# The decays' scalars and the modulation blocks move into the first three convolution groups, and the first key block is listed ahead of the decays

## The chip, the core and the metric

One NeuronCore of a Trainium2 chip runs the whole kernel in one launch. The metric is the device time of one execution in microseconds (us). TensorE (PE in the profile), VectorE (DVE), ScalarE (ACT) and GpSimd (POOL) each take their instructions in order; SyncE (SP) issues nearly all transfers, also in order. All arithmetic is float32; the projections run as three passes over a high and a low part of each operand.

## The reference, cut to what matters

One layer of a hybrid backbone, for 1024 latent tokens and 256 context tokens of width 1024:

```
mod   = silu(c) @ w_mod + b_mod                       # 6 x 1024: shift, scale, gate, twice
u     = modulate(rmsnorm(x), sh1, sc1) @ w_in         # q k v | z | b a | conformer channels
beta  = sigmoid(b);  g = -exp(a_log) * softplus(a + dt_bias)
q,k,v = silu(conv7(q,k,v)); q,k l2-normed             # 4 heads of 128
o     = gated DeltaNet over chunks, forward and backward, decays exp(sums of g)
y     = silu(layernorm(conv31 along grid columns(a * sigmoid(b'))))
x     = x + gt1 * (concat(gated_norm(o, z), y) @ w_out)
x     = x + gt2 * moe(modulate(rmsnorm(x), sh2, sc2)) # 64 experts, top 6, and a shared one
out   = rmsnorm(x) * g_final
```

## The kernel before, in words

Up to line 448 the instructions are traced in program order and a list scheduler places them: program order is priority, and what is ready may go ahead. `mod_block` (line 270) multiplies 512 columns of `w_mod` (`mod_product`, 250; 2.1 MB per block, from block 4 on through two buffers), copies the product (`ms`, 259), transposes it (265) and adds the bias (267, 268). Blocks 0 to 3 are done before the tokens are modulated. Then a loop over four groups j of 128 conformer channels (422) projects each group in two halves (`cf_project`, 368; `fm`, 314, is one projection of 24 products per 512 tokens), loads the next group's weights (`load_cf`), does two modulation blocks, 4+2j and 5+2j, and for j below 3 the 31 taps of the grid convolution (`grid_tap`, 412; tap 15 starts the sum on ScalarE, 415, the others are VectorE's, 419). After the loop the gates are laid into `gtc`, transposed, and stored to `gt_d` (434 to 448).

From line 488 on the order is planned: each step is listed with an engine, a planned duration, what it reads and writes (by names), and `Order.emit` (105) plays these through, always giving a free engine the ready step with the longest path behind it (`low` steps after all others). What is emitted is the order in each engine's queue; between the part before and this part the list scheduler still interleaves. Names of buffers and PSUM banks are dealt out in turn when a step is listed (`turn_of`, `bbank`: banks 4 to 7 in turn), so the listing decides who waits for whose buffer. The first planned part contains:

- `o_scalars` (582): two parameter loads, sigmoid and softplus of the 80 gate scalars per token on ScalarE and VectorE (587 to 601), running sums on TensorE (608 to 612), their exponentials `eg` (615), a transpose (617) and the store `egr_d` (620). Its result `gg` feeds every decay.
- `o_grid_conv(3)`: the last group's grid convolution.
- `o_decays(c)` (629) for ten chunks: masked copies of `gg` on GpSimd (637) and ScalarE (635), running sums on TensorE (643), an Exp (646), a store.
- `o_norm_half` (534): the layer norm of the conformer channels, in two halves.
- `o_qkv(blk)` (716): load and split of one weight block (683 on ScalarE, 684 on GpSimd; staging in three buffers, split parts in two, four after `open_prep`), the projection (697), copies into `cx` (723, 726), seven taps (744 on ScalarE, 746 or 710 on VectorE), Silu (752), transposes (763), and for keys the squares and their sums (767 to 769). Blocks 4 to 7 are keys, 8 to 11 values, 0 to 3 queries. `o_z` (778) is a projection without taps.
- `o_masks` (831): block masks on GpSimd and VectorE, with `low=1`.
- `o_key_norms` (649), `o_prep1` (883: products of keys, 892, times decay factors, 897 to 901), `o_spread` (911), `o_base_inverse` (924: 15 steps on VectorE, 937 and 938, on copies held in `qf`), then `o_conv_out` (786) and `o_query_norms` (952). `open_prep` closes the pool of the convolution and opens the next one.

A second planned part follows: inverses, the scan over chunks, output projection, routing and shared expert; then the routed experts, whose weights are loaded once the router's expert list is there (fetch, lines 1752 to 1775).

Of the kernel before, what the change touches and what calls it, by code (L numbers as in the profile page):

```python
# [8 lines left out]
F32 = mybir.dt.float32  # L9
# [4 lines left out]
OP = mybir.AluOpType  # L14
# [135 lines left out]
def hybrid_kernel(tc, a, out):  # L150
# [270 lines left out]

    for j in range(4):
# [12 lines left out]
    gt_d = dp.tile([32, 128], F32, name="gt_d")  # L435
    pt = bank("b")
    gtc = cfp.tile([128, 32], F32, name="gtc")
    V.tensor_copy(gtc[:, 0:8], MC[:, 16:24, 0])
    V.tensor_copy(gtc[:, 8:16], MC[:, 40:48, 0])
    for i in range(2):  # L440
        V.tensor_copy(gtc[:, 16 + 8 * i:24 + 8 * i], sv['mf'][i])
    PE.transpose(pt[0:32, 0:128], gtc, ident)
    gtr = cfp.tile([32, 128], F32, name="gtr")
    V.tensor_copy(gtr, pt[0:32, 0:128])
    SY.dma_start(gt_d, gtr)

    mf8 = cp.tile([128, 2, 8], F32, name="mf8")
    SY.dma_start(mf8, gt_d[16:32].rearrange("(a b) c -> a (b c)", a=2).rearrange("a (p k) -> p a k", k=8))
# [21 lines left out]
    egr_d = dp.tile([80, 128], F32, name="egr_d")  # L470
# [87 lines left out]

    rk = keep.tile([128, 10, 4], F32, name="rk")
    ssk = keep.tile([128, 10, 4], F32, name="ssk")  # L560
    ssq = keep.tile([128, 8, 4], F32, name="ssq")
    alb = keep.tile([128, 2, 8], F32, name="alb")
    bav = bat.rearrange("p c (d w h) -> p w d c h", d=2, w=2)

    def sct(name):
        return keep.tile([128, 2, 10, 4], F32, name=name)

    beta, gg = sct("beta"), sct("gg")
    tmp = lnp.tile([128, 2, 10, 4], F32, name="tmp")
    egr = lnp.tile([80, 128], F32, name="egr")  # L570
    eg = keep.tile([128, 3, 2, 10, 4], F32, name="eg")
    egc, egl = eg[:, 0], eg[:, 2]
# [5 lines left out]

    def per_dh(t):
        return t.rearrange("p (d h) -> p d h", d=2)[:, :, None, :].to_broadcast([128, 2, 10, 4])  # L580

    def o_scalars():
        DMA(0.3, lambda: SY.dma_start(alb[:, 0], w['dn_a_log'].rearrange("d h -> (d h)").partition_broadcast(128)),
            w=["alb0"])
        DMA(0.3, lambda: SY.dma_start(alb[:, 1], w['dn_dt_bias'].rearrange("d h -> (d h)").partition_broadcast(128)),
            w=["alb1"])
        ACT(0.3, lambda: S.activation(beta, bav[:, 0], AF.Sigmoid), w=["beta"])
        DVE(0.3, lambda: V.tensor_tensor(gg, bav[:, 1], per_dh(alb[:, 1]), op=OP.add), r=["alb1"], w=["gs"])

        def softplus():  # L590
            S.activation(tmp, gg, AF.Abs)
            S.activation(tmp, tmp, AF.Exp, scale=-1.0)
            S.activation(alb[:, 0], alb[:, 0], AF.Exp)
            S.activation(tmp, tmp, AF.Ln, bias=1.0)

        ACT(4.0, softplus, r=["alb0"], w=["gs"])

        def decay():
            V.scalar_tensor_tensor(gg, gg, 0.0, tmp, op0=OP.max, op1=OP.add)
            V.tensor_tensor(gg, gg, per_dh(alb[:, 0]), op=OP.mult)  # L600
            V.tensor_scalar(gg, gg, -1.0, None, op0=OP.mult)

        DVE(0.7, decay, w=["gs", "gg"])
        b, kb = bbank()

        def sums():
            ggf = gg.rearrange("p d c h -> p d (c h)")
            PE.matmul(b[:, 0:40], Ui, ggf[:, 0], start=True, stop=True)
            PE.matmul(b[:, 40:80], Li, ggf[:, 1], start=True, stop=True)
            PE.matmul(b[:, 80:120], Ls, ggf[:, 0], start=True, stop=True)  # L610
            PE.matmul(b[:, 120:160], Us, ggf[:, 1], start=True, stop=True)
            PE.matmul(b[:, 160:240], ones, gg.rearrange("p d c h -> p (d c h)"), start=True, stop=True)

        TE(1.2, sums, r=["gs"], w=[kb])
        ACT(1.7, lambda: S.activation(eg.rearrange("p a d c h -> p (a d c h)"), b[:, :240], AF.Exp), r=[kb], w=["eg"])
        b2_, kb2 = bbank()
        TE(0.2, lambda: PE.transpose(b2_[0:80, 0:128], egc.rearrange("p d c h -> p (d c h)"), ident), r=["eg"],
           w=[kb2])
        DVE(0.25, lambda: V.tensor_copy(egr, b2_[0:80, 0:128]), r=[kb2], w=["egr"])
        DMA(0.3, lambda: SY.dma_start(egr_d, egr), r=["egr"], w=["egrd"])  # L620

        DVE(0.3, lambda: V.tensor_reduce(Ic, ident.rearrange("p (b c) -> p c b", c=16), axis=AX.X, op=OP.add), w=["ic"])
# [6 lines left out]
    def o_decays(c):  # L629
# [7 lines left out]
        POOL(1.5, lambda: G.tensor_tensor(RR[u], bm(Ui), b3(gg[:, 0, c]), op=OP.mult), r=["gg"], w=[f"rr{u}"])  # L637
# [32 lines left out]
    def o_load_w(src, k=8, by=None, kby=None):  # L670
# [4 lines left out]
        for i in range(0, k, k // 2):  # L675
# [8 lines left out]
            POOL(1.5, lambda st=st, sl=sl: G.tensor_tensor(lo(sl), st, hi(sl).bitcast(F32), op=OP.subtract),  # L684
# [31 lines left out]
    def o_qkv(blk):  # L716
# [33 lines left out]
        for t in range(1, 7):  # L750
            DVE(1.7, lambda t=t: tap(t), r=[kc], w=[kd])
# [34 lines left out]
    def o_conv_out():  # L786

        wt = []
        for hf in range(2):
            hs_ = slice(hf * 512, (hf + 1) * 512)  # L790
            DMA(0.8, lambda hf=hf: SY.dma_start(flat(DM[hf]), gt_d[4 * hf:4 * hf + 4].rearrange("k p -> (k p)")
                                                .partition_broadcast(128)), w=[f"dm{hf}"])
            wt.append([o_load_w(w['w_out'].rearrange("(k p) n -> p k n", p=128)[:, 4 + 2 * i:6 + 2 * i, hs_], 2,
                                lambda hf=hf: flat(DM[hf]), f"dm{hf}") for i in range(2)])
        for t in range(8):
# [8 lines left out]
            POOL(1.5, lambda hs=hs, parts=parts: G.tensor_tensor(parts()[1], hs, parts()[0].bitcast(F32),  # L804
# [26 lines left out]
    def o_masks():  # L831
# [10 lines left out]
        POOL(1.8, blocks, w=["bd"], low=1)  # L842
# [10 lines left out]
        for s in (16, 32, 64):  # L853
            DVE(1.3, lambda s=s: level(s), r=["bd"], w=[f"m{s}"], low=1)
# [28 lines left out]
    def o_prep1(n):  # L883
        bounce = BN[n]
        for ci, c in enumerate(pairs[n]):
# [14 lines left out]
            POOL(1.5, lambda d=d: G.tensor_tensor(N.NB, N.NB, DM[d], op=OP.mult), r=[f"dm{d}"], w=["nb"])  # L900
# [23 lines left out]
    def o_base_inverse(n):  # L924
# [15 lines left out]
        for m0 in range(0, 15, 3):  # L940
            DVE(2.3, lambda m0=m0: steps(m0, m0 + 3), r=[*kr, "ic"], w=["xf"])
# [43 lines left out]

    def o_grid_conv(j):
        kw = [f"y{j}0", f"y{j}1"]
        ACT(1.2, lambda: grid_tap(j, 15), w=kw)
# [5 lines left out]
    TE(14.0, lambda: None)  # L994
    ACT(6.0, lambda: None)
    POOL(0.6, pads, w=["cx0", "cx1"])
    o_scalars()
    o_grid_conv(3)
    for c in pairs[0]:
        o_decays(c)  # L1000
    for c in pairs[1]:
        o_decays(c)
    for c in pairs[2]:
        o_decays(c)
    for c in pairs[3]:
        o_decays(c)
    for c in pairs[4]:
        o_decays(c)
    o_norm_half(0)
    o_norm_half(1)  # L1010
    o_qkv(4 + 0)
    o_qkv(4 + 1)
    o_qkv(4 + 2)
    o_qkv(4 + 3)
    o_masks()
    once(open_prep, w=["prep", "rv", "gs", "egr", "bd", *(f"rr{i}" for i in range(4)), *(f"y{j}{hf}" for j in range(4) for hf in range(2))])
# [21 lines left out]
    o_z(3)
# [1070 lines left out]
```

## Time and profile before

| | us |
|---|---|
| median of 3 runs | 1730.98 (1727.82 to 2079.73) |
| the profiled execution | 1729.29 |
| its span, first to last instruction | 1727.5 |
| TensorE busy in it | 1604.0 |
| VectorE, GpSimd, ScalarE busy | 977.9, 522.6, 485.3 |

The profile is of one execution. Busy time is of instructions that compute; transfers and waits are not in it. The span is shorter than the time by what lies before the first and behind the last instruction.

### The profile page before, as it was taken

The page shows a single profiled execution, that of the slowest core. Times are in us where ns is not written, and L with a number is a line of the kernel's source. Part 1 is how long each engine was busy: PE and PEld are TensorE (multiplying, and loading weights), DVE is VectorE, ACT ScalarE, POOL GpSimd, SP SyncE. Part 2 cuts the span into 40 slices and gives each one's busy share as a digit, 9 for nine tenths or more (in the row PEclk, how much of TensorE's full clock was granted, in tenths as well). Part 3 has the DMA queues.
Part 4 walks back from the last instruction along what each step waited for, and adds up shares of the span by engine and source line. Part 5 has one row for each costly group of instructions (what it writes and reads, how often), then busy time and mean ns, then how long its engine had stood idle before and what let it go on. Part 6 is the DMA issues. An engine that isn't in the chain of part 4 may idle for free. (4 is left out here: it accounts for less than half of the span.)

```text
span 1727.5 us, 23370 instructions
## 1 busy us (share of the span) xinstructions
PE 1604.0 (93%) x8380; PEld 936.3 (54%) x8380; DVE 977.9 (57%) x2156; ACT 485.3 (28%) x1085; POOL 522.6 (30%) x443
## 2 busy tenths in 40 slices
PE   5999699986998999899999999999999999999994
PEld 1556456865875899788544434344444344443441
DVE  2588865889775985878702444444444434343424
ACT  4521445742232112444212111112121112111212
POOL 2321331162222776732011222323232323232310
PEclk9999899988999999899999999999999999999998
DMA  9455121364525336666358999999999999999957
GB/s 322 152 181 173 32 86 49 112 188 141 184 72 175 96 98 196 216 208 223 140 221 292 340 325 333 315 363 316 322 380 362 333 334 319 321 385 350 353 131 250
DMA packets 150657, 405.38 MB, mean 235 GB/s; under 512 B 21360, under 2 KB 64781, under 8 KB 125581
## 3 DMA queue, kind: packets, MB, share of 16 engines
q1 hardware_dynamic: 130978, 340.39, 54.2%
q0 software_dynamic: 18288, 59.26, 14.5%
q10 hardware_dynamic: 1274, 4.23, 0.6%
q8 instruction: 66, 1.08, 0.2%
q14 instruction: 51, 0.41, 0.1%
HBM read 340.01 MB, written 71.95 MB: 238 GB/s over the span
## 5 line engine op out<-in xcount | busy, mean ns | idle before, releaser
L1607 PE MATMUL gu<-wg,hg 128*32 128x512 f32 (+2 forms) x1968 | 463.2, 599 | 1.8 <-ACT hg L1861 1.8
L1886 DVE SCALAR_TENSOR_TENSOR ob<-dn,wc,gt2b 128x512 f32<-128x512 f32 x124 | 93.1, 751 | 366.0 <-PE dn L1627 366.0
L1895 POOL DMA_INDIRECT acc<-ob,ic x89 | 134.5, 1512 | 527.5 <-DVE st L1817 467.1
L1607 PEld LDWEIGHTS gu<-wg,hg 128*32 128x32 f32 (+2 forms) x1968 | 148.4, 137 | 204.3 <-issue 159.2
L1627 PE MATMUL dn<-wd,sg 128*32 128x512 f32 (+2 forms) x984 | 226.8, 597 | 0.5 <-ACT sg L1618 0.5
L1861 ACT ACTIVATE hg<-xt,mf 128x128 f32<-128x128 f32 x248 | 93.2, 456 | 377.6 <-PE xt L1855 376.0
L1627 PEld LDWEIGHTS dn<-wd,sg 128*32 128x32 f32 (+2 forms) x984 | 77.8, 137 | 143.5 <-issue 142.7
L697 PE MATMUL bk<-hTh,whi 128*128 128x512 f32 (+1 forms) x320 | 127.3, 398 | 8.4 <-ACT ot L783 4.3
L697 PE MATMUL bk<-hTh,wlo 128*128 128x512 f32 (+1 forms) x320 | 121.2, 379 | 0.5 <-POOL wlo L684 0.5
L697 PE MATMUL bk<-hTl,whi 128*128 128x512 f32 (+1 forms) x320 | 121.4, 379 | 0.0
L1859 DVE TENSOR_SCALAR hg<-xt,mf 128x128 f32<-128x128 f32 x248 | 84.3, 402 | 52.1 <-DMA acc<-hg 52.0
L419 DVE SCALAR_TENSOR_TENSOR ycv<-yg,cfw,ycv 128x64 f32<-128x64 f32 (+14 forms) x120 | 107.6, 896 | 5.3 <-ACT ycv L415 2.0
L684 POOL TENSOR_TENSOR wlo<-wst,whi 128x512 fp32r<-128x512 f32 x40 | 65.3, 1637 | 134.1 <-ACT whi L683 134.1
L1845 POOL DMA_INDIRECT xg<-xn_d,ig x62 | 76.6, 1236 | 65.1 <-issue 19.7
L697 PEld LDWEIGHTS bk<-hTh,whi 128*128 128x128 f32 x320 | 62.1, 194 | 32.9 <-issue 11.6
L1806 DVE TENSOR_TENSOR oh<-posl 128x1024 bf16<-128x1024 f32 (+3 forms) x89 | 77.6, 897 | 0.0
L1855 PE MATMUL xt<-ident,xg 128*128 128x128 f32 x496 | 70.3, 285 | 0.0
L697 PEld LDWEIGHTS bk<-hTh,wlo 128*128 128x128 f32 x320 | 62.0, 194 | 12.6 <-POOL wlo L684 0.9
L697 PEld LDWEIGHTS bk<-hTl,whi 128*128 128x128 f32 x320 | 62.1, 194 | 11.5 <-issue 1.4
L1612 DVE TENSOR_TENSOR sg<-sg,gu 128x256 f32<-128x256 f32 x62 | 26.1, 421 | 63.6 <-ACT sg L1611 63.6
L1611 ACT ACTIVATE sg<-gu 128x256 f32<-128x256 f32 x62 | 23.8, 383 | 135.1 <-PE gu L1607 135.1
L1855 PEld LDWEIGHTS xt<-ident,xg 128*128 128x128 f32 x496 | 60.3, 194 | 1.4 <-issue 1.4
(444 smaller groups left out, 2661.1 us busy)
## 6 DMA issues: line engine op xcount, KB each, us to landing
wg<-exp_w_gate SPq DMA_DIRECT2D x64, 1024.0 KB
wg<-exp_w_up SPq DMA_DIRECT2D x64, 1024.0 KB
wd<-exp_w_down SPq DMA_DIRECT2D x64, 1024.0 KB
wm<-w_mod SPq DMA_DIRECT2D x24, 1024.0 KB
wst<-w_in SPq DMA_DIRECT2D x48, 256.0 KB
kv<-kv_d SPq DMA_DIRECT2D x20, 512.0 KB
qf<-bounce SPq DMA_DIRECT2D x20, 256.0 KB
eb<-egr_d SPq DMA_DIRECT2D x18, 256.0 KB
```

The costliest lines, as they stand in the source:

```text
L419: V.scalar_tensor_tensor(yc[:, lo:hi], yg[:, lo + d:hi + d], cfw[:, t * 4 + j:t * 4 + j + 1], yc[:, lo:hi], op0=OP.mult, op1=OP.add)
L684: POOL(1.5, lambda st=st, sl=sl: G.tensor_tensor(lo(sl), st, hi(sl).bitcast(F32), op=OP.subtract), r=[ks_, kh_], w=[kl_])
L697: PE.matmul(b[:, :n], l(k), r[:, k, t0:t0 + n], start=(k == 0 and i == 0), stop=(k == 7 and i == 2))
L1607: PE.matmul(pgu[o:o + n, :].rearrange("p (a f) -> p a f", a=2), lhsT(k, o, n), wts[r][0][:, :, k, :], start=(k == 0), stop=(k == 7), tile_ ...
L1627: PE.matmul(pd[o:o + n, :], aT[:, k, o:o + n], wts[r][1][:, k, hf * 512:(hf + 1) * 512], start=(k == 0), stop=(k == 1), tile_position=(0, ...
L1806: V.tensor_tensor(oh[:, :, o:o + n], N.iol[:, None, p0:p0 + n].to_broadcast([128, 8, n]), N.posr[:, :, r:r + 1].to_broadcast([128, 8, n]), ...
L1845: G.indirect_dma_start(out=xg, out_offset=None, in_=xn_d, in_offset=bass.IndirectOffsetOnAxis(ap=ig, axis=0), bounds_check=1023, oob_is_er ...
L1855: PE.transpose(pt[:, csl(q)], nth(B['xg'][:, 0:1024], 4 * j + q, 8), ident)
L1859: V.tensor_scalar(hg[:, k, :], pt[:, csl(q)], sc_[:, k:k + 1], sh_[:, k:k + 1], op0=OP.mult, op1=OP.add)
L1861: S.activation(hg[:, k, :], pt[:, csl(q)], AF.Identity, scale=sc_[:, k:k + 1], bias=sh_[:, k:k + 1])
L1886: V.scalar_tensor_tensor(ob[:, hs_], res[hf], B['wc'], N.gt2b[:, hs_], op0=OP.mult, op1=OP.mult)
L1895: G.indirect_dma_start(out=acc_d[turn[0]], out_offset=bass.IndirectOffsetOnAxis(ap=ic[:n], axis=0), in_=B['ob'][o:o + n], in_offset=None, ...
```

## The change

`o_scalars` is no longer planned: the same instructions are a function `scalars()` called in the loop's group j=1, ahead of its modulation blocks. Blocks 4 to 11 are done as 4, 5, 6 / 7, 8, 9 / 10, 11 / none. The gates become a listed step `o_gates` that waits for the first key block (`kf0`), and so do the masks, now without `low`. Two empty steps stand for TensorE's and VectorE's remaining work ahead of the plan. Key blocks, decays and norms are listed in another order, and so are some value, z and preparation steps. Planned durations of some steps are changed.

```diff
+    def scalars():
+        SY.dma_start(alb[:, 0], ...)
+        SY.dma_start(alb[:, 1], ...)
+        S.activation(beta, bav[:, 0], AF.Sigmoid)
+        V.tensor_tensor(gg, bav[:, 1], per_dh(alb[:, 1]), op=OP.add)
+        S.activation(tmp, gg, AF.Abs)
+        S.activation(tmp, tmp, AF.Exp, scale=-1.0)
+        S.activation(alb[:, 0], alb[:, 0], AF.Exp)
+        S.activation(tmp, tmp, AF.Ln, bias=1.0)
...
+        b = bank("b")
...
+        S.activation(eg.rearrange("p a d c h -> p (a d c h)"), b[:, :240], AF.Exp)
+        b2_ = bank("b")
+        PE.transpose(b2_[0:80, 0:128], egc.rearrange("p d c h -> p (d c h)"), ident)
+        V.tensor_copy(egr, b2_[0:80, 0:128])
+        SY.dma_start(egr_d, egr)
...
-        for n in (4 + 2 * j, 5 + 2 * j):
+        if j == 1:
+            scalars()
+        for n in ((4, 5, 6), (7, 8, 9), (10, 11), ())[j]:
             mod_block(n)
...
-    scale_shift('mf', 'g_ffn', 32, 24, 0)
-    pt = bank("b")
-    gtc = cfp.tile([128, 32], F32, name="gtc")
...
-    SY.dma_start(gt_d, gtr)
-    SY.dma_start(mf8, ...)
...
-        POOL(1.5, ...)                # decays, weight splits, factors, output parts
+        POOL(1.6, ...)
-            DVE(1.7, lambda t=t: tap(t), r=[kc], w=[kd])
+            DVE(1.6 if kind == 1 else 1.9, lambda t=t: tap(t), r=[kc], w=[kd])
-        POOL(1.8, blocks, w=["bd"], low=1)
+        DVE(0.3, lambda: V.tensor_reduce(Ic, ...), r=["kf0"], w=["ic"])
+        POOL(1.8, blocks, r=["kf0"], w=["bd"])
-            DVE(1.3, lambda s=s: level(s), r=["bd"], w=[f"m{s}"], low=1)
+            DVE(1.3, lambda s=s: level(s), r=["bd"], w=[f"m{s}"])
-            DVE(2.3, lambda m0=m0: steps(m0, m0 + 3), r=[*kr, "ic"], w=["xf"])
+            DVE(2.8, lambda m0=m0: steps(m0, m0 + 3), r=[*kr, "ic"], w=["xf"])
+    def o_gates():
...
+        DVE(0.7, columns, r=["kf0"], w=["gtc"])
+        TE(0.3, lambda: PE.transpose(b[0:32, 0:128], gtc, ident), r=["gtc"], w=[kb])
+        DVE(0.3, lambda: V.tensor_copy(gtr, b[0:32, 0:128]), r=[kb], w=["gtr"])
+        DMA(0.3, lambda: SY.dma_start(gt_d, gtr), r=["gtr"], w=["gtd"])
+        DMA(0.3, lambda: SY.dma_start(mf8, ...), r=["gtd"])
...
-        ACT(1.2, lambda: grid_tap(j, 15), w=kw)
+        ACT(1.2, lambda: grid_tap(j, 15), r=["yg"], w=kw)
-    TE(14.0, lambda: None)
-    ACT(6.0, lambda: None)
+    TE(7.0, lambda: None, w=["yg"])
+    DVE(0.7, lambda: None, w=["yg"])
-    o_scalars()
```

The listing, before and after (D are the decays of a pair, N the norm halves, K, V, Q the blocks of `o_qkv`, P `o_prep1`, S `o_spread`, I `o_base_inverse`, Z `o_z`):

```
before: scalars, grid 3, D0 D1 D2 D3 D4, N0 N1, K0 K1 K2 K3, masks | P0 S0 P1 S1 V0 P2 V1 P3
        V2 I0 S2 V3 Z0 I1 S3 Z1 I2 Z2 I3 Z3 Q0 P4 S4 Q1 I4 Q2 Q3
after:  grid 3, K0, D0 D1, N0 N1, K1, gates, D2, K2, D3, K3, masks, D4 | P0 S0 P1 S1 V0 P2 V1 P3
        I0 V2 S2 Z0 I1 S3 V3 Z1 I2 P4 S4 Z2 I3 Q0 I4 Z3 Q1 Q2 Q3
```

## Rows read from the trace of the kernel before

**Rows 1.** The page: the span, part 1 (busy us, share of the span, instructions) and, from part 2, the DMA share in tenths in 40 equal slices.

```profile
span 1727.5 us, 23370 instructions
...
PE 1604.0 (93%) x8380; PEld 936.3 (54%) x8380; DVE 977.9 (57%) x2156; ACT 485.3 (28%) x1085; POOL 522.6 (30%) x443
...
DMA  9455121364525336666358999999999999999957
```

**Rows 2.** The table by stretch (us): busy us of each engine with its instructions, mean granted clock of TensorE (1 is the full clock), share of the 16 DMA engines, GB/s.

```profile
183.20:202.90 19.70, 6.12 (x43) 1.98 (x42) 13.14 (x44) 9.04 (x15) 3.13 (x8) 0.71 0.06 15
202.90:338.70 135.80, 133.94 (x587) 92.31 (x587) 92.27 (x85) 78.93 (x147) 34.17 (x23) 0.98 0.26 79
338.70:431.00 92.30, 69.07 (x336) 57.42 (x336) 83.76 (x121) 34.84 (x62) 41.75 (x24) 0.87 0.58 163
431.00:556.00 125.00, 122.72 (x504) 93.12 (x504) 83.99 (x142) 37.60 (x60) 30.95 (x21) 0.98 0.43 140
960.00:1000.00 40.00, 40.00 (x256) 15.95 (x252) 15.79 (x48) 6.88 (x19) 9.94 (x7) 1.00 1.00 334
```

**Rows 3.** TensorE's timeline around the end of the last group: start us, us from the first start to the last end, line, operation, tiles, shapes, count, and in brackets the idle time before it and who ended it.

```profile
183.17 2.76 PE L256 MATMUL a<-wm,csil 128*32 128x512 f32 x18
185.87 0.66 PE L265 MATMUL b<-ident,ms 128*128 128x128 f32 x4
186.46 1.92 PE L256 MATMUL a<-wm,csil 128*32 128x512 f32 x14
189.14 0.66 PE L265 MATMUL b<-ident,ms 128*128 128x128 f32 x4 [0.77 <-ACT ms L259]
190.55 0.28 PE L442 MATMUL b<-ident,gtc 128*32 128x128 f32 x1 [0.75 <-DVE gtc L439]
202.89 0.62 PE L608 MATMUL bk<-gg,Ui 128*128 128x40 f32 x2 [12.06 <-DVE gg L601]
...
204.59 0.69 PE L612 MATMUL bk<-gg,ones 128*128 128x80 f32 x2
205.02 0.77 PE L697 MATMUL bk<-hTh,whi 128*128 128x512 f32 x1
```

**Rows 4.** VectorE's timeline in the same stretch, same columns (the lines left out between the grid taps are those of the masks, 848 to 851).

```profile
192.37 0.23 DVE L588 TENSOR_TENSOR gg<-bat,alb 128x80 f32<-128x80 f32 x1
192.52 0.48 DVE L419 SCALAR_TENSOR_TENSOR ycv<-yg,cfw,ycv 128x256 f32<-128x256 f32 x1
...
194.25 0.54 DVE L419 SCALAR_TENSOR_TENSOR ycv<-yg,cfw,ycv 128x320 f32<-128x320 f32 x1
...
195.98 0.61 DVE L419 SCALAR_TENSOR_TENSOR ycv<-yg,cfw,ycv 128x384 f32<-128x384 f32 x1
...
198.84 3.24 DVE L419 SCALAR_TENSOR_TENSOR ycv<-yg,cfw,ycv 128x448 f32<-128x448 f32 x4
202.00 0.23 DVE L599 SCALAR_TENSOR_TENSOR gg<-gg,tmp 128x80 f32<-128x80 f32 x1
...
202.54 0.20 DVE L601 TENSOR_SCALAR gg<-gg 128x80 f32<-128x80 f32 x1
```

**Rows 5.** ScalarE's timeline: the softplus with its function-table loads, and the first Silu of the planned part.

```profile
192.93 1.28 ACT L592 ACT_TABLE_LOAD   x1
194.22 0.27 ACT L592 ACTIVATE tmp<-tmp 128x80 f32<-128x80 f32 x1
...
195.90 0.27 ACT L594 ACTIVATE tmp<-tmp 128x80 f32<-128x80 f32 x1
...
256.85 1.28 ACT L752 ACT_TABLE_LOAD   x1
```

**Rows 6.** The table by stretch behind the wait, columns as in rows 2.

```profile
202.90:206.00 3.10, 3.10 (x12) 2.93 (x13) 3.03 (x3) 3.08 (x9) 3.10 (x2) 0.50 0.00 0
206.00:209.00 3.00, 3.00 (x8) 1.91 (x7) 2.96 (x2) 1.42 (x3) 3.00 (x3) 0.60 0.00 0
209.00:212.00 3.00, 3.00 (x10) 1.45 (x9) 2.93 (x3) 2.01 (x6) 3.00 (x2) 1.00 0.47 109
```

**Rows 7.** TensorE's timeline at the modulation blocks of the first three groups: the transposes of a block (265) with their waits, and the product of the first group's second block (256).

```profile
93.79 0.66 PE L265 MATMUL b<-ident,ms 128*128 128x128 f32 x4 [0.23 <-ACT ms L259]
94.38 1.92 PE L256 MATMUL a<-wm,csil 128*32 128x512 f32 x14
...
125.23 0.65 PE L265 MATMUL b<-ident,ms 128*128 128x128 f32 x4 [3.76 <-ACT ms L259]
...
156.60 0.66 PE L265 MATMUL b<-ident,ms 128*128 128x128 f32 x4 [3.02 <-ACT ms L259]
```

**Rows 8.** The table by stretch while the two blocks of the second group are loaded, columns as in rows 2.

```profile
93.00:96.50 3.50, 3.27 (x23) 1.30 (x22) 2.15 (x7) 1.87 (x3) 0.00 (x0) 1.00 0.59 174
96.50:100.00 3.50, 3.50 (x18) 2.85 (x18) 2.70 (x8) 0.45 (x1) 0.00 (x0) 1.00 1.05 397
```

**Rows 9.** TensorE's instructions in 338.7 to 431 grouped by line: count, busy us and mean ns of one, idle time before them and who ended most of it.

```profile
L763 PE MATMUL bk<-ident,ac 128*128 128x128 f32 x40 | 7.8, 339 | 14.7 <-DVE tm L937 6.3 <-DVE ot L772 4.3 <-DVE wt L901 2.4
```

**Rows 10.** VectorE's groups in 331 to 431: the taps of the value blocks, columns as in rows 9.

```profile
L746 DVE SCALAR_TENSOR_TENSOR ac<-cx,cnv,ac 128x1283 f32<-128x1283 f32 x24 | 46.1, 1948 | 2.6 <-ACT ac L744 2.5
```

**Rows 11.** VectorE's groups in 183 to 340: the taps of the key blocks and of the last grid convolution.

```profile
L746 DVE SCALAR_TENSOR_TENSOR kf<-cx,cnv,kf 128x1283 f32<-128x1283 f32 x24 | 37.7, 1583 | 20.2 <-ACT kf L744 19.9
L419 DVE SCALAR_TENSOR_TENSOR ycv<-yg,cfw,ycv 128x64 f32<-128x64 f32 (+14 forms) x30 | 32.6, 1085 | 0.8
```

More of the change, by code (lines that the diff above doesn't have):

```diff
@@ L577, in hybrid_kernel @@
     Ic = gbase.tile([128, 16], F32, name="Ic")
[L579 to L622, printed above, removed]
@@ L840, in blocks @@
                                 channel_multiplier=-1)
-        POOL(1.8, blocks, w=["bd"], low=1)
+        DVE(0.3, lambda: V.tensor_reduce(Ic, ident.rearrange("p (b c) -> p c b", c=16), axis=AX.X, op=OP.add),
+            r=["kf0"], w=["ic"])
+        POOL(1.8, blocks, r=["kf0"], w=["bd"])
         def level(s):
@@ L984, in pads, with columns @@
                 G.memset(cx[:, z0:z0 + 3], 0.0)
+    def o_gates():
+        gtc = lnp.tile([128, 32], F32, name="gtc")
+        gtr = lnp.tile([32, 128], F32, name="gtr")
+        def columns():
+            scale_shift('mf', 'g_ffn', 32, 24, 0)
+            V.tensor_copy(gtc[:, 0:8], MC[:, 16:24, 0])
+            V.tensor_copy(gtc[:, 8:16], MC[:, 40:48, 0])
+            for i in range(2):
+                V.tensor_copy(gtc[:, 16 + 8 * i:24 + 8 * i], sv['mf'][i])
+        DVE(0.7, columns, r=["kf0"], w=["gtc"])
+        b, kb = bbank()
+        TE(0.3, lambda: PE.transpose(b[0:32, 0:128], gtc, ident), r=["gtc"], w=[kb])
+        DVE(0.3, lambda: V.tensor_copy(gtr, b[0:32, 0:128]), r=[kb], w=["gtr"])
+        DMA(0.3, lambda: SY.dma_start(gt_d, gtr), r=["gtr"], w=["gtd"])
+        DMA(0.3, lambda: SY.dma_start(mf8, gt_d[16:32].rearrange("(a b) c -> a (b c)", a=2)
+                                      .rearrange("a (p k) -> p a k", k=8)), r=["gtd"])
     def o_grid_conv(j):
         kw = [f"y{j}0", f"y{j}1"]
-        ACT(1.2, lambda: grid_tap(j, 15), w=kw)
+        ACT(1.2, lambda: grid_tap(j, 15), r=["yg"], w=kw)
         for t in range(31):
@@ L1002, in hybrid_kernel @@
         o_decays(c)
+    o_norm_half(0)
+    o_norm_half(1)
+    o_qkv(4 + 1)
+    o_gates()
     for c in pairs[2]:
         o_decays(c)
+    o_qkv(4 + 2)
     for c in pairs[3]:
         o_decays(c)
+    o_qkv(4 + 3)
+    o_masks()
     for c in pairs[4]:
         o_decays(c)
[L1009 to L1016, printed above, removed]
+    once(open_prep, w=["prep", "rv", "gtc", "gtr", "bd", *(f"rr{i}" for i in range(4)), *(f"y{j}{hf}" for j in range(4) for hf in range(2))])
     N.wbufs, turns["w"], turns["ot"] = 4, -1, 0
@@ L1026, in hybrid_kernel @@
     o_prep1(3)
+    o_base_inverse(0)
     o_qkv(8 + 2)
-    o_base_inverse(0)
     o_spread(2)
-    o_qkv(8 + 3)
     o_z(0)
@@ L1033, in hybrid_kernel @@
     o_spread(3)
+    o_qkv(8 + 3)
     o_z(1)
     o_base_inverse(2)
+    o_prep1(4)
+    o_spread(4)
     o_z(2)
     o_base_inverse(3)
+    o_qkv(0)
+    o_base_inverse(4)
     o_z(3)
-    o_qkv(0)
-    o_prep1(4)
-    o_spread(4)
     o_qkv(1)
-    o_base_inverse(4)
     o_qkv(2)
```

58 lines of the change are left out of this document (32 added, 26 removed).

## The prediction

> **What bounds the kernel now.** I read the page's busy shares first: TensorE is busy 1604.0 of 1727.5 us, VectorE 57%; and in the slices the DMA share is high only in the last half [rows 1]. So there are two kernels in one. The table by stretch says which is which: from 960 us on DMA runs at 1.00 of its engines, and before that TensorE is the fullest engine, with one hole: in 183.2 to 202.9 it is busy for 6.12 of 19.70 us, at a mean granted clock of 0.71. In 202.9 to 338.7 it is busy 133.94 of 135.80 and in 431 to 556 122.72 of 125.00; between them, 338.7 to 431, it is busy only 69.07 of 92.30, and there VectorE, with 83.76, is the fuller [rows 2]. The change works in the hole and reorders the stretches behind it. The reader should see that what is saved there reaches the end: TensorE is full in 431 to 556, the second planned part starts when that is done, and expert loads need the router's result, so all that comes later moves as one block.
>
> In the hole, TensorE's own timeline shows two modulation blocks (products 183.17 and 186.46, transposes 185.87 and 189.14), one transpose for the gates at 190.55, then 12.06 us of nothing until L608, released by VectorE's L601 [rows 3]. VectorE reaches L588 at 192.37 and L599 only at 202.00: the softplus on ScalarE was done at about 196.2, but in VectorE's order masks and seven grid taps stood ahead of L599 [rows 4, 5]. So the wait is a matter of order on VectorE, not of work. The first projection of the first key block follows at 205.02 [rows 3].
>
> **The change part by part.** Times are against the profiled execution, 1729.29 us (span 1727.5 and 1.8 around it); the median of the runs shown, 1730.98, is 1.7 above it.
>
> 1. *The wait on the scalars.* The scalars are traced at the second group (j=1), where their inputs (all token blocks are modulated by then) already exist, so `gg` is ready long before the planned part. The 12.06 us wait goes: +12.06 [rows 3]. What is late next is nothing of TensorE's own: weights of the first key block sit in a slot freed half a projection earlier, and cast and split can run under the last projection.
>
> 2. *Modulation blocks 10 and 11.* Groups of (2,2,2,2) become (3,3,2,0). The products and transposes of two blocks (2.76+0.66+1.92+0.66 = 6.0 us) move ahead of the last projection, at no net cost to a full TensorE. The two small waits around them go: 0.77 and 0.75, +1.52 [rows 3].
>
> 3. *Clock.* After the hole the granted clock is 0.50 for 3.1 us and 0.60 for 3.0 us, then 1.00, with TensorE busy throughout [rows 6]. If it is not idle, 3.1x0.50 + 3.0x0.40 = 2.75 us come back: +2.75.
>
> 4. *What the moved work costs where it lands.* TensorE takes its instructions in order, and in groups 0 and 1 its projections are now followed by a third block, in group 1 also by the scalars' ten small products and one transpose. Nearest rows: a block's transposes waited for their copy 0.23 us in the first group, but 3.76 and 3.02 in the second and third, where ScalarE's copy stood behind a grid tap that waited for VectorE [rows 7]. A third block has a further wait: only two buffers exist, so its load starts when the group's first block is multiplied; 2.1 MB at 174 GB/s up to 96.5 and 397 after it are in at about 100.2 [rows 8]. Put straight behind the second block, whose product ended at 94.38 + 1.92 = 96.3 [rows 7], it would make TensorE wait 3.9 us. Ends: nothing (the scheduler puts projections between) to 3.9 + 2x3.76 + 2x3.76 = 18.9 us for two extra blocks and the scalars' two steps. I take 3, nearer the lower end, since in the first group, where VectorE had no backlog, the row is 0.23. SP's queue gets the store of `egr_d` among the block loads: it waits for a VectorE copy, and loads behind it wait too; that is within the same ends. The two parameter loads were issued early before and stay early.
>
> 5. *First key block ahead of the decays.* Banks are dealt out in listing order, so the three transposes of key block 0 now take banks 4 to 6, decay 0 bank 7, and decay 1 waits for bank 4, thus for the whole convolution of key block 0. TensorE meanwhile has the projections of key blocks 1 and 2. Against that, the Exps of the decays, which before were listed ahead of every key block (the first Silu loads its table only at 256.85), now mix with Silu and Sqrt. Each change of function set is a table load of 1.28 us [rows 5]. I reckon four more, half of them covered: -2.6; ends 0 and -6.
>  The Trainium skill, "ScalarE: Activation LUTs", section "What ACT_TABLE_LOAD costs", puts a switch at 1.28 us of load plus about 1.38 of drain, 2.66 in all; rows 5 agree on the load but show the next activation 0.01 us behind it and no drain. By the page this term would be -5.3 and the sum 13.0; it is a rule against this order, and the row decides here.
>
> 6. *Masks and gates.* The masks leave the hole: between the grid taps at 192.52, 194.25, 195.98 and 198.84 they took 1.25+1.19+2.25 = 4.7 us of VectorE [rows 4]. They come after key block 0 instead, when VectorE waited 20.2 us ahead of key taps, 19.9 of it for their first tap on ScalarE [rows 11]: hidden, and if that cover is gone 4.7 us of VectorE. The gates' copies, transpose and two DMAs (a few tenths each) go into the planned part, needed only by the output projection: nothing. SP no longer holds the `gt_d` store at its head while waiting for the gates; nothing urgent was behind it, so nothing.
>
> 7. *Planned times and the listing from the value blocks on.* A value tap is now 1.9 in the plan (was 1.7; measured mean 1.948 [rows 10]), an inverse step of three 2.8 (2.3), a POOL split 1.6 (1.5). The instruction counts don't change. In the stretch 338.7 to 431 TensorE idles 23.2 us, 14.7 of it ahead of the transposes of value blocks [rows 2, 9]; read as transposes that stand too early in its order, they would give way to other work. Longer planned times put them later, behind projections of z and q that need nothing from VectorE; block 4's preparation and inverse come earlier. Ends: all of 23 recovered, or the 14.7 doubled by a worse order. I take +5: VectorE is 91% busy there, so most of the wait is VectorE's work, not order.
>
> Sum: 12.06 + 1.52 + 2.75 - 3 - 2.6 + 5 = 15.7 us, so 1729.3 - 15.7 = 1713.6.
>
> **Rivals.**
> (A) *VectorE takes the bound over.* With two more blocks (6.0 us) and the scalars (the small products take 2.1 at half clock, so about 1 at the full one) ahead of it, the last projection ends some 7 us later than its 183.2, so the last group's grid taps still start near 192, as they did [rows 4]. Taps (32.6 us), key taps (37.7) and the two norms then run to the same moment, and TensorE gets its hole back before the first products of keys. For it: in 338.7 to 431 VectorE is 91% full [rows 2]. Against: 20.2 us of its waits in 183 to 340 stand ahead of key taps, whose projection now comes some 12 us earlier [rows 11]. Price: of the 15.7 about 5 are left: 1724, 1721 to 1730.
> (B) *The middle closes as well.* Most of the 23.2 us go: 15.7 + 15 gives 1699, 1693 to 1706. Against: the VectorE share again.
> (C) *Slower: the third block stalls the projections.* TensorE waits in groups 0 to 2 for a load, for ms copies behind grid taps and for the scalars' chain, which now competes with a group's taps on VectorE (32.6 us in the last one). It decides from 16.3 us of new waiting before the last projection's end, the sum of terms 1 to 3; at the 18.9 of term 4 plus 6 of term 5, without term 7, the result is 16.3 - 24.9 = -8.6, so 1738, and up to 1753 if the value transposes wait longer too. For it: the 3.76 and 3.02; against: the 0.23.
> (D) The change not doing what it says would mean that the scheduler still leaves the scalars to the end. The scheduler fills gaps as soon as something is ready, as the masks between the grid taps show [rows 4], so I hold this for a small part of (A).
>
> **How the numbers follow.** Forecast (1706 to 1721) 0.50, (A) with (D) 0.25, (B) 0.13, (C) 0.12. The range reaches to 1699 below, about half of (B), and to 1734 above, about a third of (C): 0.86 or so. A measurement of this kernel tells about 2% from no change; that is below 1696.4 or above 1765.6. A quarter of (B) lies below the one, so 0.03; for a sixth of (C), where its stalls add to (A)'s, I allow the other, 0.02; the rest is within: 0.95.
>
> **What would show it.** Right: no wait of TensorE over 2 us between the end of the last projection of the conformer channels and the first of key block 0, a granted clock near 1.00 there, that first key projection near 193 rather than 205, the small products of `gg` before 150 us, and the end of the first planned part near 541 instead of 556. Term 4 is wrong if TensorE's waits before 190 grow by more than 6 us; term 5 if it waits over 4 us for decays or key transposes; term 7 if its idle time between the first key products and the last z projection doesn't fall. The prediction as a whole is wrong if the first planned part ends no earlier than at 553.

## The result and the profile after

| | us |
|---|---|
| before, median | 1730.03 |
| after, median of 5 runs | 1718.88 (1717.08 to 1720.67) |
| ratio | 0.994, 95% interval 0.9924 to 0.9956 |
| the profiled execution after | 1718.04 (before 1729.29) |

By the ratio the change saves 10.4 us of 1730 (7.6 to 13.1), 0.6%. The time lies inside the forecast's 1706 to 1721, near its slow end; the forecast gain of 15.7 lies outside the measured interval. One of the five runs before was a slow one (2079.73 us), and the ratio compares the others. The profile after, against [rows 1]:

```profile
span 1716.1 us, 23373 instructions
...
PE 1599.0 (93%) x8380; PEld 931.8 (54%) x8380; DVE 974.5 (57%) x2156; ACT 498.4 (29%) x1096; POOL 526.2 (31%) x443
```

TensorE and VectorE execute the same number of instructions as before; ScalarE has 11 more and 13.1 us more to do. Of this page, that is what points at the loss. TensorE is busy 5.0 us less for the same 8380 products, at a mean granted clock over the whole execution of 0.975 instead of 0.970: not all of the gain is idle time.

The lines of the code have shifted: a projection is now L676 (was 697), the transposes of a convolved block L742 (763), key products L873 (892), VectorE's scaling of the value blocks by the key norms L751 (772), z's Silu L762, the key and value Silu L731 (752), an Exp of a decay L625 (646), the layer norm's Sqrt and Silu L589 and L593 (550, 554), key norms L629 to L631. The table by stretch, columns as in [rows 2]:

```profile
183.20:189.50 6.30, 6.30 (x29) 5.23 (x28) 6.12 (x6) 3.00 (x8) 2.92 (x2) 1.00 0.06 15
189.50:202.90 13.40, 13.40 (x72) 11.51 (x70) 11.59 (x17) 3.71 (x6) 4.11 (x3) 1.00 0.34 92
280.00:320.00 40.00, 30.73 (x119) 17.42 (x118) 17.78 (x25) 33.98 (x60) 8.75 (x6) 0.89 0.35 111
338.70:431.00 92.30, 71.61 (x360) 58.94 (x358) 80.76 (x131) 30.48 (x53) 32.41 (x21) 0.91 0.55 152
```

The hole of [rows 2] is closed: from 183.2 to 202.9 TensorE is busy throughout at granted clock 1.00. A new one has opened a hundred us later, in 280 to 320, where it is idle for 9.3 us, the mean granted clock is 0.89, and the fullest engine is ScalarE, with 34.0 of 40 us. Before, this stretch had no hole (nor had the whole of 202.9 to 338.7, [rows 2]):

```profile
280.00:320.00 40.00, 40.00 (x202) 30.46 (x201) 28.57 (x25) 23.39 (x37) 5.14 (x4) 1.00 0.26 73
```

TensorE's timeline after, columns as in [rows 3]; it answers to [rows 3, 7]:

```profile
97.08 0.66 PE L265 MATMUL b<-ident,ms 128*128 128x128 f32 x4 [0.71 <-ACT ms L259]
98.40 1.07 PE L256 MATMUL a<-wm,csil 128*32 128x512 f32 x8 [0.66 <-DMA wm<-w_mod]
...
122.96 0.31 PE L461 MATMUL b<-gg,Ui 128*128 128x40 f32 x2
...
127.96 0.66 PE L265 MATMUL b<-ident,ms 128*128 128x128 f32 x4 [0.70 <-ACT ms L259]
...
134.42 1.94 PE L256 MATMUL a<-wm,csil 128*32 128x512 f32 x8 [2.53 <-DMA wm<-w_mod]
...
189.06 0.39 PE L320 MATMUL a<-hTh,wlo 128*128 128x512 f32 x1
189.29 0.39 PE L676 MATMUL bk<-hTh,whi 128*128 128x512 f32 x1
```

The first projection of a key block follows the last one of the conformer channels without a gap, 15.7 us earlier than the 205.02 of [rows 3]; the products of `gg` run at 122.96. The third blocks do wait for their loads, but for 0.66 and 2.53 us, and the copies are waited for 0.7 us, not the 3.76 and 3.02 of [rows 7].

In the stretch with the new hole, TensorE's waits (the bracket again) and ScalarE's timeline show one thing from both sides:

```profile
290.87 0.44 PE L742 MATMUL bk<-ident,kf 128*128 128x128 f32 x2 [0.95 <-ACT dm L625]
...
299.95 1.10 PE L622 MATMUL bk<-rrp,Ls 128*128 128x512 f32 x2 [1.51 <-ACT dm L625]
...
305.54 0.44 PE L742 MATMUL bk<-ident,kf 128*128 128x128 f32 x2 [0.83 <-ACT dm L625]
307.27 1.83 PE L622 MATMUL bk<-rrp,Ls 128*128 128x512 f32 x2 [1.29 <-ACT dm L625]
...
312.51 1.16 PE L873 MATMUL bk<-kf 128*128 128x128 f32 x8 [1.12 <-ACT dm L625]
316.86 2.05 PE L622 MATMUL bk<-rrp,Ls 128*128 128x512 f32 x2 [3.19 <-ACT ot L746]
```

```profile
286.99 1.28 ACT L589 ACT_TABLE_LOAD   x1
288.28 0.63 ACT L589 ACTIVATE rv<-rv 128x512 f32<-128x512 f32 x1
288.93 1.28 ACT L625 ACT_TABLE_LOAD   x1
290.22 0.60 ACT L625 ACTIVATE dm<-bk 128x512 f32<-128x512 f32 x1
...
294.14 1.28 ACT L731 ACT_TABLE_LOAD   x1
295.43 1.27 ACT L731 ACTIVATE kf<-kf 128x1283 f32<-128x1283 f32 x1
296.61 0.80 ACT L593 ACTIVATE ycv<-ycv,vec 128x512 f32<-128x512 f32 x1
...
297.91 1.28 ACT L625 ACT_TABLE_LOAD   x1
299.20 0.60 ACT L625 ACTIVATE dm<-bk 128x512 f32<-128x512 f32 x1
299.82 1.28 ACT L593 ACT_TABLE_LOAD   x1
301.12 0.81 ACT L593 ACTIVATE ycv<-ycv,vec 128x512 f32<-128x512 f32 x1
```

The bank of a decay is given back by its Exp, and the next user of the bank, of whatever kind, waits for it. Nearly every Exp, Silu and Sqrt here finds another function's table loaded, so a 0.6 us activation costs 1.9.

### The profile page after: what moved, and what is told of

Same layout as the page of the kernel before. It is cut to its first block, busy times and chain, and to the rows that moved or that the text cites. A ratio compares the mean times of both kernels' runs of the same rounds, so it can differ in the third digit from the quotient of the medians.

```text
span 1716.1 us, 23373 instructions
## 1 busy us (share of the span) xinstructions
PE 1599.0 (93%) x8380; PEld 931.8 (54%) x8380; DVE 974.5 (57%) x2156; ACT 498.4 (29%) x1096; POOL 526.2 (31%) x443
## 5 line engine op out<-in xcount | busy, mean ns | idle before, releaser
L676 PE MATMUL bk<-hTh,whi 128*128 128x512 f32 (+1 forms) x320 | 125.0, 391 | 12.2 <-ACT ot L762 9.4
L676 PE MATMUL bk<-hTl,whi 128*128 128x512 f32 (+1 forms) x320 | 120.0, 375 | 0.0
L676 PE MATMUL bk<-hTh,wlo 128*128 128x512 f32 (+1 forms) x320 | 119.8, 374 | 0.0
L419 DVE SCALAR_TENSOR_TENSOR ycv<-yg,cfw,ycv 128x64 f32<-128x64 f32 (+14 forms) x120 | 103.5, 863 | 5.7 <-ACT ycv L415 2.7
L676 PEld LDWEIGHTS bk<-hTh,whi 128*128 128x128 f32 x320 | 61.3, 192 | 32.4 <-ACT ot L762 9.8
L676 PEld LDWEIGHTS bk<-hTl,whi 128*128 128x128 f32 x320 | 61.5, 192 | 10.8 <-issue 1.0
L676 PEld LDWEIGHTS bk<-hTh,wlo 128*128 128x128 f32 x320 | 61.2, 191 | 11.2
```

What stands on the lines that cost most here:

```text
L419: V.scalar_tensor_tensor(yc[:, lo:hi], yg[:, lo + d:hi + d], cfw[:, t * 4 + j:t * 4 + j + 1], yc[:, lo:hi], op0=OP.mult, op1=OP.add)
L676: PE.matmul(b[:, :n], l(k), r[:, k, t0:t0 + n], start=(k == 0 and i == 0), stop=(k == 7 and i == 2))
```

## The experiments

Three marks are read in every trace besides the time: TensorE's idle time from the last projection of the conformer channels to the key norms (before 13.58 us, after 12.45), its idle time from there to the second planned part (30.77, 28.86), and the start of that part, its first transposes (559.40, 549.51). One execution can lie some us from the median, so a mark is compared with the mark of another profiled execution, a median with a median. How far a mark repeats can be seen from four traces with the same order up to the key norms (the changed kernel and the last three below): 12.45, 12.48, 13.98 and 13.99 us for the first, and key norms between 317.0 and 318.6. A difference of under some 2 us in a mark says nothing by itself.

**All decays ahead of the key blocks**, everything else as in the changed kernel:

```diff
     o_grid_conv(3)
+    for pair in pairs:
+        for c in pair:
+            o_decays(c)
     o_qkv(4 + 0)
-    for c in pairs[0]:
-        o_decays(c)
...
```

> All ten decays are listed ahead of key block 0; the rest is the changed kernel. Function-table loads of ScalarE in the first planned part fall from 17 to 8 by the order. Theory T (the mixing of Exp with Silu and Sqrt costs TensorE its lead): TensorE's idle time from the end of the conformer projections to the key norms falls from 12.5 us to under 5, key norms near 307 instead of 317.0, second planned part's first transposes near 541 instead of 549.5, time 1708 to 1712. Rival R1 (key block 0 first is what VectorE needs, the loads are covered): key norms at 317 or later, time 1718 or more. Rival R2 (waits for banks and VectorE, whatever the order): no difference, 1716 to 1720.

Measured 1713.37 (1705.17 to 1717.09, 6 runs), ratio 0.9896 (0.9873 to 0.9919): 18.0 us below before, and its interval and that of the changed kernel don't touch. The time lies between theory T's 1708 to 1712 and R2's 1716, nearer to T. The first idle mark fell from 12.45 to 3.10, the second part starts at 543.09. ScalarE's loads of function tables from 189 to 541 (line, count, busy us and mean ns) and the stretch of the hole (columns as in [rows 2]):

```profile
L731 ACT ACT_TABLE_LOAD x2 | 2.6, 1283 | 0.0
L589 ACT ACT_TABLE_LOAD x2 | 2.6, 1283 | 0.0
L593 ACT ACT_TABLE_LOAD x2 | 2.6, 1283 | 0.0
L625 ACT ACT_TABLE_LOAD x1 | 1.3, 1283 | 0.0
```

```profile
280.00:320.00 40.00, 40.00 (x213) 31.64 (x213) 30.63 (x33) 24.69 (x41) 3.90 (x2) 1.00 0.27 80
```

The changed kernel, in the same view:

```profile
L625 ACT ACT_TABLE_LOAD x7 | 9.0, 1283 | 0.1
L731 ACT ACT_TABLE_LOAD x5 | 6.4, 1283 | 0.1
...
L593 ACT ACT_TABLE_LOAD x3 | 3.8, 1283 | 0.1
...
L589 ACT ACT_TABLE_LOAD x2 | 2.6, 1283 | 0.0
```

Ten loads fewer (both have one more each at L631 and L282, so 9 instead of 19) and TensorE full again in that stretch. The key norms missed their mark, 319.0 instead of some 307. TensorE was not idle for it: between the last conformer projection and the key norms it does 419 products of projections (L676) instead of the changed kernel's 384 and 40 of the decays' instead of 37, so in this order more work stands ahead of them. The run moves the order as well as the loads, so alone it doesn't say which of the two helps; the next one does.

**One function set**, the order untouched:

```diff
-        ACT(0.6, lambda: S.activation(RV, RV, AF.Sqrt), w=["rv"])
+        ACT(0.6, lambda: S.activation(RV, RV, AF.Tanh), w=["rv"])
...
-        ACT(2.0, lambda: S.activation(dst(), dst(), AF.Silu), w=[kd])
+        ACT(2.0, lambda: S.activation(dst(), dst(), AF.Tanh if kind == 1 else AF.Silu), w=[kd])
```

> The changed kernel with its order kept, but Silu of the key blocks, Silu of the conformer norm and its Sqrt are computed as Tanh, which shares a table with Exp: 17 loads of function tables in the first planned part become 3. The output is another one, so routing and the experts' time may differ; read up to the start of the second planned part. Theory T: TensorE's idle time up to the key norms falls from 12.5 to under 5 us, key norms near 306, second part's first transposes near 540. Rival R2 (order, banks, VectorE): idle stays over 10, key norms 315 or later.

With another result the routing differs, so its total time (2738.94) says nothing; up to the second planned part it is comparable. The Silu of the conformer norm (593) is replaced as well. The loads of L589 and L593 are gone and one each is left at L625 and L731, so 4 loads instead of 19. The first idle mark is 5.14, the key norms come at 307.8 (after: 317.0), the second part at

```profile
541.12 1.12 PE L1084 MATMUL bk<-ident,et 128*128 128x128 f32 x4 [4.37 <-DVE et L1108]
```

against 549.51: with the order untouched, 15 loads fewer are worth 8.4 us there, in one execution of each. Idle is a little over the "under 5" that was written down; the theory's other marks were met within 2 us.

**The moves without the new listing**: the kernel before with the scalars in group j=1, blocks (3,3,2,0) and the two empty steps, its own listing and planned times kept.

```diff
+        if j == 1:
+            scalars()
-        for n in (4 + 2 * j, 5 + 2 * j):
+        for n in ((4, 5, 6), (7, 8, 9), (10, 11), ())[j]:
...
-    o_scalars()
```

> The kernel before with only the scalars moved to group 1 and the modulation blocks in groups of 3, 3, 2, 0; listing, gates, masks and planned times as before (the two empty steps as in the changed kernel). Theory T (the moves carry the gain, the new listing gives part of it back): 1710 to 1716, faster than the changed kernel's 1718.9 by 3 or more. Rival R1 (the new listing is needed to use the lead): 1722 to 1729.

Measured 1719.77 (1717.81 to 1725.33), ratio 0.994 (0.992 to 0.996): between the two expectations, both missed. The same ratio as the whole change, so the new listing, taken as one, gave no net gain in time. Its profiled execution was a long one (1723.42), with the second part at 554.8. It has only the 8 loads that the kernel before has without the scalars, so something else holds it. Its first key projection starts at 193.06, 12.0 us earlier than before; behind its last conformer projection TensorE's waits are (columns as in [rows 9], 187.9 to 324)

```profile
L638 PE MATMUL bk<-rrp,Ls 128*128 128x512 f32 x20 | 10.6, 613 | 2.9 <-POOL rrp L632 2.9
...
L578 PE MATMUL bk<-ycv,ones 128*32 128x512 f32 x16 | 9.2, 662 | 4.4 <-DVE ycv L419 4.4
```

that is, the decays' sums wait for GpSimd's masked copies and the layer norm's sums for VectorE's last grid taps. In the changed kernel the first of these is gone and the second is 2.5 us. So the new listing both gives and takes; the first two experiments show what it takes.

**The scalars alone, the blocks alone.**

```diff
-        for n in ((4, 5, 6), (7, 8, 9), (10, 11), ())[j]:
+        for n in (4 + 2 * j, 5 + 2 * j):
```

> e3_moves_only with the modulation blocks left in groups of 2, 2, 2, 2: only the scalars are moved. By terms 1 to 4 of the prediction the scalars carry nearly all of the gain and the blocks at most 1.5 us: 1719 to 1723. Rival: the blocks matter, since two of them at the end of the last group delay the first key projection by 6 us without cover: 1724 to 1728.

The run before with the blocks back at two per group: 1722.13, ratio 0.9958 (0.9945 to 0.9972), 7.3 us below before, as expected.

> The kernel before with the modulation blocks in groups of 3, 3, 2, 0 and nothing else. The wait on the scalars stays on VectorE, so TensorE's hole only grows by the 6 us that blocks 10 and 11 filled: 1727 to 1733, no gain. Rival: with the blocks gone from the end, VectorE reaches the scalars' end earlier and the hole shortens: 1720 to 1726.

The kernel before with only the blocks moved: 1727.11 (12 runs), ratio 0.9979 (0.9967 to 0.9991), 3.6 us below before. A small gain where none was expected: the two small waits of term 2 are gone, and in its trace the first key projection comes at 203.31, 1.7 us earlier than before. 7.3 + 3.6 = 10.9 agrees with the 10.4 of both together, each of these within some 2 to 4 us, so nothing here shows that one move needs the other; the wait on the scalars is the larger share.

**The old second half** in the changed kernel: listing from the value blocks on, and planned times, as before the change.

```diff
-            DVE(1.6 if kind == 1 else 1.9, lambda t=t: tap(t), r=[kc], w=[kd])
+            DVE(1.7, lambda t=t: tap(t), r=[kc], w=[kd])
...
-            DVE(2.8, lambda m0=m0: steps(m0, m0 + 3), r=[*kr, "ic"], w=["xf"])
+            DVE(2.3, lambda m0=m0: steps(m0, m0 + 3), r=[*kr, "ic"], w=["xf"])
```

> The changed kernel with the listing behind the second preparation step and the planned times of before. My prediction's term 7 (+5 us for the changed kernel): 1722 to 1726. Theory T (TensorE's idle time in the middle is the same 28.9 us in both traces, so the middle listing gave nothing): 1717 to 1721.

Measured 1716.24 (1713.44 to 1718.68), ratio 0.9913 (0.9896 to 0.9929), a little below what had been expected; the second part starts at 548.6, with 26.37 us idle in the middle instead of 28.86. The old listing is no worse and, with intervals that just overlap, perhaps a few us better. The +5 forecast for the new one isn't there. The waits are in other places, though: ahead of the value blocks' transposes (317 to 549, columns as in [rows 9]) the changed kernel has none and this one 12.5 us, near the 14.7 of [rows 9].

```profile
L742 PE MATMUL bk<-ident,ac 128*128 128x128 f32 x40 | 5.8, 275 | 0.0
```

```profile
L742 PE MATMUL bk<-ident,ac 128*128 128x128 f32 x40 | 7.8, 347 | 12.5 <-DVE tm L918 6.6 <-DVE ot L751 3.4 <-DVE wt L882 2.6
```

**Decays first and the old second half together** (both diffs above).

> All decays listed ahead of key block 0 (as in e1_decays_first), and the listing behind the second preparation step and the planned times of before (as in e4_old_middle). If the two effects are separate, 1713.4 less some 2.7: 1709 to 1712. If the old middle only helps where the table loads had delayed the key norms: 1713 to 1716, no better than e1_decays_first.

Measured 1712.01 (1708.80 to 1713.48), ratio 0.9899 (0.9885 to 0.9912); second part at 541.18. The time lies at the upper end of the first expectation and below the second. This and the first experiment are the fastest versions, below both kernels; between the two of them no difference can be seen, so what the old middle adds to decays first is not shown.

**The middle, with less for VectorE to do**: 12 of the 15 steps of each base inverse left out.

```diff
-            for m in range(m0, m1):
+            for m in range(m0, m1 if m0 == 0 else m0):
```

> The changed kernel with 12 of the 15 steps of each base inverse left out (they are planned as before, so the order is kept; the output is another one, so read up to the start of the second planned part). If VectorE's work is what TensorE waits for in the middle, its idle time between key norms and second part falls from 28.9 us to under 15 and the second part starts before 537. If the order of the value and key products is (transposes and products that stand too early): idle stays over 24.

VectorE's idle time in the middle rose from 56.2 to 94.5 us, TensorE's fell only from 28.86 to 26.35, and the second part starts at 550.2. So VectorE's amount of work by itself doesn't set the wait. The second expectation's number, over 24, is met; its reason, the order, this run doesn't test. In the changed kernel the waits of that stretch (317 to 549; columns as in [rows 9]) name ScalarE's Silu of z beside VectorE's scaling of the value blocks:

```profile
L676 PE MATMUL bk<-hTh,whi 128*128 128x512 f32 (+1 forms) x192 | 76.9, 401 | 12.2 <-ACT ot L762 9.4 <-ACT cx L705 2.8
...
L799 PE MATMUL bk<-whi,hcr 128*128 128x512 f32 x128 | 41.1, 401 | 0.8 <-POOL hcr L783 0.8
...
L873 PE MATMUL bk<-kf 128*128 128x128 f32 x72 | 11.1, 303 | 11.5 <-DVE ot L751 10.2 <-DVE wt L882 1.3
```

The table of all engines' waits for the same stretch adds where L762, z's Silu, stands:

```profile
ACT ot L762 <- DMA kv_d<-ot: 19.5, 3, 11.2
```

(total us, times, the longest). z and the value blocks share two buffers `ot`; z's Silu waits for a value block's store, and the projection behind it for the bank.

**z with buffers of its own.**

```diff
-            o = turn_of("ot", 2)
-            ACT(1.2, lambda b=b, o=o: S.activation(flat(OT[o]), b, AF.Silu), r=[kb], w=[f"ot{o}"])
+            o = turn_of("zt", 2)
+            ACT(1.2, lambda b=b, o=o: S.activation(N.ZT[o], b[:, :64], AF.Silu), r=[kb, "prep"], w=[f"zt{o}"])
```

> The changed kernel with two buffers of their own for the Silu of the z projections (778 before, 762 after). For want of room each holds 64 of the 512 columns, and the store writes them eight times, so the other columns of z are left out and the result differs; read only up to the start of the second planned part. In the changed kernel ScalarE's Silu of z waits 19.5 us in three places for stores of value blocks out of the two buffers that both use, and behind it TensorE waits 9.4 us ahead of projections. Theory T (the shared buffers hold TensorE): those waits of L762 on stores of value blocks are gone, TensorE's idle time between the key norms and the second planned part falls from 28.9 to 18 to 23 us, and that part starts at 540 to 545 instead of 549.5. Rival R (VectorE's products and taps are late in any case, the waits only change their place): the idle time stays above 25 and the start at 547 to 552. ScalarE also has some 3 us less to do in Silu, which is too little for the one or the other.

```profile
L676 PE MATMUL bk<-hTh,whi 128*128 128x512 f32 (+1 forms) x192 | 75.0, 391 | 0.0
...
L799 PE MATMUL bk<-whi,hcr 128*128 128x512 f32 x128 | 45.4, 435 | 17.2 <-ACT cx L705 9.6 <-DVE nb L803 6.1 <-POOL hcr L783 1.5
...
L874 PE MATMUL bk<-kf 128*128 128x128 f32 x72 | 9.4, 281 | 3.1 <-DVE wt L883 3.0
```

The waits named by the theory are gone, 12.2 and 11.5 us become 0.0 and 3.1, and yet the rival has the time: 25.67 us idle, second part at 547.1. 17.2 us have appeared ahead of the conformer channels' part of the output projection (`o_conv_out`), 9.6 of it behind ScalarE's copy of a query block, which in the table of waits stands for a query block's taps on VectorE (L689):

```profile
ACT cx L705 <- DVE qf L689: 20.3, 2, 13.9
```

**Both at once**, by the two diffs above.

> The run before with, in addition, 12 of the 15 steps of each base inverse left out as in the run with the short inverse (so z and the inverses are incomplete, the result differs; read only up to the start of the second planned part). Each of the two alone lowered TensorE's idle time between the key norms and the second planned part by about 3 us only (28.9 to 26.4 with the short inverse, to 25.7 with z apart, where the waits of projections and key products were gone but 17.2 us appeared ahead of the products of the output projection, 9.6 of it behind ScalarE's copy of a query block that waited for VectorE's taps). Theory T (two limits side by side, the shared buffers and VectorE's amount of work: taking away one leaves the other): with both gone the idle time falls to 8 to 16 us and the second part starts at 530 to 538. Rival R (the order of the steps, or ScalarE and the transfers, hold TensorE whatever VectorE and the buffers do): idle stays above 21 and the start at 543 to 549.

```profile
L676 PE MATMUL bk<-hTh,whi 128*128 128x512 f32 (+1 forms) x192 | 75.0, 391 | 0.0
...
L799 PE MATMUL bk<-whi,hcr 128*128 128x512 f32 x128 | 45.2, 433 | 10.5 <-ACT cx L705 6.3 <-POOL hcr L783 3.2 <-DVE nb L803 0.9
```

Idle 18.47, second part at 539.96: neither expectation. Singly 2.5 and 3.2 us, little more than the 2 us by which a mark repeats; together 10.4. The two limits cover each other, as one theory had it, but 18 us stay with the shared buffers gone and VectorE's work cut down. What holds those is open.

## Why the prediction was right in direction and too large

The forecast names its steps; here they are against the two traces. The step that was off most is term 5, a mechanism that was seen and mis-sized; term 7's gain didn't come either.

*Terms 1 to 3 (the wait, the small waits, the clock, +16.3): held at the place they are about.* No wait over 2 us between the last conformer projection and the first key projection, granted clock 1.00, the products of `gg` at 122.96 (forecast: before 150). Singly, with the old listing, the scalars are worth 7.3 us of the whole time and the blocks 3.6: in that listing too a part of the lead is lost behind this place.

*Term 4 (new waits, -3): too careful.* The first key projection was forecast near 193 and came at 189.29. TensorE's idle time from 94.4 to the last conformer projection didn't grow; it fell from 6.78 to 5.37. The third blocks' loads cost 0.66 and 2.53, but the two gaps of 3.76 and 3.02 in [rows 7] are gone as well. With the stretch of lower clock behind the wait, of which 1.7 us lay behind the old first key projection (0.50 x 0.98 + 0.40 x 3.0, by [rows 6]), the lead is 15.7 + 1.7 = 17.4 us, an estimate; terms 1 to 4 had 13.3.

*Term 5 (table loads, -2.6): the step that failed.* The mechanism was named and its size was wrong: the count. Forecast were four more loads, half of them covered. Without the scalars' own four, before had 8 from the conformer channels to the second part, after has 19: 11 more, x 1.283 = 14.1 us. The half was about right: ten loads fewer (12.8 us of ScalarE) bring the second part 6.4 us forward in the first experiment and the median 5.5 us down, and 15 fewer (19.2 us) are worth 8.4 in the second. So 11 loads come to some 5 to 8 us, an estimate, around the lower end of the range for this term (-6). The prediction doesn't say how it came to four. In the listing decays stand beside key blocks in a handful of places, but the planner has no cost for a change of tables: it takes the ready step with the longest path, and the trace shows Exp, Silu and Sqrt one by one. The prediction's own sign for this, over 4 us of waiting for decays and key transposes, is in the trace: the five waits on L625 shown add up to 5.7 us, and 3.19 follow behind a copy that stood in the same queue.

The Trainium skill, "ScalarE: Activation LUTs", section "Table sets: the hidden batching unit", gives the rule that was broken: batch activations by set, not by function. The traces agree: with the decays listed in one piece, 9 loads instead of 19 come with 5.5 us less. No run shows the drain that the Trainium skill's section "What ACT_TABLE_LOAD costs" of the same page adds to a load; the next activation starts 0.01 us behind it.

*Term 7 (middle listing, +5): not there.* The middle's idle time fell by 1.9 us, from 30.77 to 28.86, and with the old listing it is 26.37. By the sign that the prediction named, TensorE's idle time from the first key products (334.0 before, 312.5 after) to the last z projection (456.4, 468.9), it didn't fall: 25.2 us before, 26.9 after, in a longer stretch. Part of the mechanism did happen: the value blocks' transposes stand at other places in TensorE's order and the 14.7 us ahead of them are gone, while the old listing has 12.5 of them again. But the waits moved: ahead of projections stand 12.2 us (8.4 before), 9.4 of them behind z's Silu and the buffers that it shares with the value blocks, and ahead of key products 11.5 (1.9 before), 10.2 of them behind VectorE's scaling of the value blocks. What failed is that the work put in front was to "need nothing from VectorE". Without the shared buffers and with less for VectorE to do, 10.4 us of the wait go, singly about 3; the rest is open.

The sum at the second planned part: 17.4 of lead, 8.4 lost to table loads, 0.9 from the rest (the one-set run leads by 559.4 - 541.1 = 18.3), which makes 9.9; from there to the end the profiled executions differ by 1.4 more. The 8.4 is that run's 15 loads; whether the four among them that the kernel before has as well cost anything, no run shows. Read the other way, from 94.4 us to this place TensorE is idle 4.4 us less (51.1 to 46.7) and busy 5.5 us less (413.9 to 408.4): more than half of the 9.9 is products that run faster, at a mean granted clock of 0.98 instead of 0.94 between the last conformer projection and the key norms. The first planned part's last products end at 545.1 instead of 555.0; the prediction had 541 for 556, and its test for being wrong as a whole, no end before 553, doesn't apply.

That the time lies inside the range is in part luck: against the forecast, term 4 came out 4.1 us better, term 5 some 5.8 worse (by the 8.4) and term 7's 5 us are missing. The small rests, 0.9 and 1.4, were not forecast.

*The rivals.* (A) had the right shape, the hole comes back ahead of the first key products, at a price of 1721 to 1730 that the measured time undercuts, with the wrong engine: in 280 to 320 VectorE is busy for 17.8 of 40 us and ScalarE for 34.0. VectorE's last grid taps hold TensorE for 2.5 us in the changed kernel, and for 4.4 in the run with the moves alone. (B) asked for the middle to close; it didn't. (C) didn't happen: the stalls of the third block stayed under 3 us each. (D) is excluded by the 122.96.

## What to carry to other kernels

When a change lets chains with different activation functions run side by side, count the table loads in the order that a queue will really have, not in the listing, and list each set's work in one piece; the 5.5 us between the medians of the changed kernel and of the version with the decays first come with ten loads fewer. A wait that is taken away at one place can come back at another: here 17 us of lead at the first key projection are 10 at the second planned part. After a gain, read the same marks further down, and read busy time at the granted clock beside idle time. A wait that is gone from one line of the table, as the one ahead of the value blocks' transposes, is no gain until the sum of all lines has fallen. Where several limits lie side by side, taking one away shows little, and that little is no proof that it was not a limit.

## What the runs showed of the hardware

A change of function set takes 1.283 us in every one of these rows, whichever set it is, and the next activation starts 0.01 us after it. Silu, Sqrt and Exp each reload the tables after one another, while copies and squares between them need no load; Silu of the key blocks and of the layer norm share theirs (296.61 follows 295.43 without a load), and with Tanh in place of these Silus and the norm's Sqrt the ten Exps of the decays need one load instead of seven. Exp and Ln of the softplus each load [rows 5], and in the kernel before the Exp behind that Ln loads again (L615 at 205.24). TensorE's clock: behind the 12 us wait the granted clock was 0.50, the lower of its two levels (1.2 GHz), in 202.9 to 206.0 [rows 6]; in the changed kernel, where TensorE had no idle time from 183.2 on, it was 1.00 (2.4 GHz) throughout 183.2 to 202.9.
